# A residual's loads, activations' stores, two low parts of a column and one projection, moved to other queues, another engine, an earlier place

## The chip, the cores and the metric

One of the eight cores of a Trainium2 chip runs the whole program. Its engines are TensorE (PE, with PEld for its weight loads), VectorE (DVE), ScalarE (ACT), GpSimd (POOL) and SyncE (SP, which only issues DMAs). ScalarE and GpSimd can issue DMAs too, each on a queue of its own. The metric is the device time of one execution in microseconds (us), from the inputs in the chip's memory to the outputs in it.

## What is computed

Two transformer blocks on one sequence of 1024 tokens of width 1024, in float32. The change touches the second one:

```
h = rmsnorm(x, attn_norm)
q, k, v, g, gk_low, s5_u, rg_x, rg_gate = split(h @ w_in)
y_gla = gla_mixer(q, k, v, g, gk_low, ...)      # 4 heads, chunks of 64 tokens, decay per key feature
y_s5  = rmsnorm(s5_mixer(s5_u, ...))
y_rg  = rmsnorm(rglru_mixer(rg_x, rg_gate, ...))
x = x + concat(y_gla, y_s5, y_rg) @ w_out
h = rmsnorm(x, mlp_norm)
x = x + conv_ffn(h, w_up, conv_w, conv_b, w_down)
out = rmsnorm(x, final_norm)

def rglru_mixer(xr, gate, ...):
    xc = causal_dwconv(xr, conv_w, conv_b)
    r, i = sigmoid(xc @ w_a + b_a), sigmoid(xc @ w_x + b_x)      # per head
    a = exp(-8 * r * softplus(-lam))
    h_t = a_t * h_(t-1) + sqrt(1 - a_t**2) * i_t * xc_t
    return h * gelu(gate)

def conv_ffn(h, w_up, conv_w, conv_b, w_down):                   # 1024 -> 2 x 2816 -> 1024
    up, gv = split(h @ w_up)
    return (gelu(causal_dwconv(up, conv_w, conv_b)) * gv) @ w_down
```

The first block (two attentions, then a mixture of 16 experts) runs ahead of it.

## The kernel before, in words

A float32 product is made as three matmuls of rounded parts: each operand x is split into a high part h (rounded, a CAST or copy on ScalarE) and a low part l = x - h (a subtraction, most often on VectorE), and `mm3` issues h*h, h*l and l*h (lines 260 to 262). The high part is what PE waits for first, then the low part.

**Order.** The code is recorded operation by operation, and each engine then runs its own list in order; what stands in the lists is shown below where the change moves it. A DMA waits in its issuing engine's list, so whatever stands behind a waiting DMA waits too. Eight completion semaphores are taken in turn by the DMAs of the SP and ACT queues together: a DMA that takes one waits first until the previous DMA on it has landed.

**Mixers** (`mix_small`, from about 1100 to 1230 us of the span). PE makes the low-rank decay (`pgl`), then `gla_decays` for the first pair of heads: two products `pgk` (L1669), gz, Abs, Exp and Ln on ScalarE (L1670 to 1674), a scan on VectorE that makes gb, and a store of it to `qk_d` (L1678). Then come the eight products `prg` of the RG-LRU gates (L1538), each followed by a tanh into `rgg` on ScalarE (L1539), and RG-LRU's chain (L1544 to 1561). `gla_qk(0, 0)` and `gla_qk(0, 1)` are the projections of q and k for the first pair of heads: 48 matmuls each in two halves of 24, with a copy `qo` on ScalarE (L1689) and a store to `qk_d` on GpSimd's queue. Then S5's output product `pglu` (L1574) and `gla_decays` for the second pair. In `gla_out`, quad 0 loads q, k and gb back, takes exponentials `gx` on ScalarE (L1732), makes `gkd`, `QH`, `QT` on VectorE, and goes on with small matmuls (`pkd`, `sc`, `kv`, `po`). GpSimd clears QH, QT, KD and ST beforehand with twelve memsets (L1707).

**Handover** (`cols`, about 1395 to 1438 us). When a 128-token block j of the second half (j = 4 to 7) is normalised (`xn`, L269), PE transposes it (`pt`, L1894), and four sums of blocks are made with the rows of the first half (`rb`): t[0] (L1912), t[1] (L1913), t[2] (L1915) on VectorE, t[3] (L1916) on GpSimd. Each, and the block itself, is split: high part on ScalarE (L1899), low part on VectorE (L1900): XT2, XT3, XT1, XT4, X22. Up's first new product, `pb`, reads XT2.

**Up** (about 1433 to 1851 us). Seven products of half-size blocks take the place of eight, in 22 steps i; steps 2g and 2g + 1 make group g of eleven. `act(i)` multiplies gelu(up) by gv (L2220) into `ft` and stores parts of it to `act_d` (L2222, L2236, L2237); GpSimd makes sums of blocks (`block_sums`, L1980 to 1983) and stores them too (L2240 to 2242). GpSimd also makes the sums of the next weights (L2176 to 2184) and of Down's weights (L2227 to 2230).

**Down** (about 1851 to 2095 us). Seven products of eleven units. A unit is one tile `wraw` of two 256 KB loads, activations (L2033) and weights (L2034), then split into `whi` (L1999, ScalarE) and `wlo` (L2000, VectorE). The residual x3 comes into `res` in sixteen pieces of 256 KB (`piece`, L2025); product 0's call of `piece` after every second unit spreads them over the first products. The first CAST of Down writes into room that tiles of Up's activations held, so it waits for their last stores.

Of the kernel before, what the change touches and what calls it, by code (L numbers as in the profile page):

```python
# [7 lines left out]
F32 = mybir.dt.float32  # L8
# [4 lines left out]
OP = mybir.AluOpType  # L13
# [173 lines left out]
class K:  # L187
# [1232 lines left out]
    def mix_small(self, ps, st, XH, XL):  # L1420

        nc, a, V = self.nc, self.a, self.nc.vector
        from contextlib import ExitStack
        rg = self.pool(st, "rgwork")
        qk = self.pool(st, "qkwork", side="right")
# [78 lines left out]
        for q in range(4):  # L1504
# [13 lines left out]
            y = wb.tile([128, 4, 128], F32, tag="y5", name="y5", bufs=2)  # L1518
# [7 lines left out]
        gl, gu, gb, cm = self.gla_low(ps, qk, XH, XL)  # L1526
        self.gla_decays(ps, qk, 0, gl, gu, gb, cm)

        wr = rg.tile([128, 2, 2, 128], F32, name="rgw")
        nc.sync.dma_start(wr, a["rg_w"])  # L1530
        G = []
        for i in range(2):
            G.append([rg.tile([128, 1024], F32, tag=f"rgg{m}", name="rgg", bufs=2) for m in range(2)])
            for m in range(2):
                for n in range(2):
                    c = slice(512 * n, 512 * n + 512)
# [15 lines left out]
        for i in range(2):  # L1552
# [6 lines left out]
            V.tensor_tensor_scan(out=h, data0=t, data1=xc[i], initial=0.0, op0=OP.mult, op1=OP.add)  # L1559
            V.tensor_tensor(xc[i], h, GT[i], op=OP.mult)  # L1560
            nc.gpsimd.dma_start(self.yS[2 + i], xc[i])
        for t in range(2):
            self.gla_qk(ps, qk, XH, XL, 0, t)

        yf = [room("uf", "yf") for _ in range(2)]
        for i in range(2):
# [126 lines left out]
    def gla_out(self, ps, lw, ms, XH, XL):  # L1693
# [192 lines left out]
        def cols(xn, j):  # L1886


            c = slice(128 * (j % 4), 128 * (j % 4) + 128)
            pts = []  # L1890
            for q in range(2):
                pt = ps.tile([128, 4, 128], F32, tag="tr", name="pt", bufs=2)
                for d in range(4):
                    nc.tensor.transpose(pt[:, d], xn[:, 512 * q + 128 * d:512 * q + 128 * d + 128], self.ident)  # L1894
                pts.append(pt)

            def split(n, x):
                h, l = (t[:, :, c] for t in self.X[n])
                nc.scalar.copy(h, x)  # L1899
                V.tensor_tensor(l, x, h.bitcast(F32), op=OP.subtract)  # L1900
            if j < 4:
                r = wk.tile([128, 2, 4, 128], F32, tag="rb", name="rb", bufs=1)
                for q, n in enumerate(("11", "21")):
                    split(n, pts[q])
                    nc.scalar.copy(r[:, q], pts[q])
                nc.sync.dma_start(self.xr_d[j], r.rearrange("p q k t -> p (q k t)"))
                return
            b11, b21 = (raw[j][:, q] for q in range(2))
            p12, p22 = pts
            t = [ow.tile([128, 4, 128], F32, tag="yr", name="xt", bufs=4) for _ in range(4)]  # L1910
            nc.scalar.copy(t[3], p12)
            V.tensor_tensor(t[0], p12, b11, op=OP.subtract)  # L1912
            V.tensor_tensor(t[1], p22, t[0], op=OP.subtract)  # L1913
            split("T2", t[1])
            V.tensor_tensor(t[2], p22, t[3], op=OP.subtract)  # L1915
            nc.gpsimd.tensor_tensor(t[3], b21, t[1], op=OP.subtract)  # L1916
            split("T3", t[2])
            split("T1", t[0])
            split("T4", t[3])
            split("22", p22)  # L1920
            if j < 6:
                fetch(j + 2)
# [85 lines left out]
    def ffn_down(self, st, out):  # L2008
# [13 lines left out]
        def piece():  # L2022
            if pieces:
                j, c = pieces.pop(0)
                nc.sync.dma_start(res[:, j, c], self.x3_d[128 * j:128 * j + 128, c])  # L2025
        wdown = a["wdown"]
        second = {0: lambda g: wdown[g, :, n0], 1: lambda g: wdown[g + 11, :, n0], 2: lambda g: wdown[g + 11, :, n1]}
        for i, k in ((4, 0), (5, 1), (6, 2), (3, 3)):
# [21 lines left out]
        def product(i, P, start=False):  # L2050
            for g in range(11):
                w = unit(i, g)
                if g % 2:
                    piece()
                for t in range(4):
                    mms(P[t], w, t, start and g == 0, g == 10)
# [60 lines left out]
class Up:  # L2117
# [98 lines left out]
    def act(self, i):  # L2216
        nc, a, G, k, A = self.nc, self.a, self.nc.gpsimd, self.k, self.A
        t0, t1 = self.T0, self.T1
        g = i // 2
        nc.vector.tensor_tensor(A[i], A[i], self.U[i][1], op=OP.mult)  # L2220
        if i % 2 == 0:
            nc.sync.dma_start(k.act_d[0, g], A[i][:, t0])  # L2222

            r0, r1 = self.pair()
            nc.sync.dma_start(r0, a["wdown"][g])
            nc.sync.dma_start(r1, a["wdown"][g + 11])
            G.tensor_tensor(r0[:, t0], r0[:, t1], r0[:, t0], op=OP.subtract)  # L2227
            G.tensor_tensor(r0[:, t1], r1[:, t1], r0[:, t1], op=OP.subtract)
            G.tensor_tensor(r1[:, t1], r1[:, t1], r0[:, t0], op=OP.subtract)
            G.tensor_tensor(r1[:, t0], r1[:, t0], r1[:, t1], op=OP.subtract)  # L2230
            for x, n in ((r0, (0, 2)), (r1, (3, 1))):
                for c, m in zip((t0, t1), n):
                    nc.sync.dma_start(k.wdt_d[m, g], x[:, c])
            return
        x, y = A[i - 1], A[i]
        nc.sync.dma_start(k.act_d[1, g], y[:, t0])  # L2236
        nc.sync.dma_start(k.act_d[3, g], y[:, t1])  # L2237
        s12, s34 = self.pair()
        k.block_sums(G, s12, s34, x[:, t0], y[:, t0], x[:, t1], y[:, t1])
        G.dma_start(k.act_d[4:6, g].rearrange("i p c -> p i c"), s12.rearrange("p (i c) -> p i c", i=2))  # L2240
        G.dma_start(k.act_d[6, g], s34[:, t0])
        G.dma_start(k.act_d[2, g], s34[:, t1])
# [104 lines left out]
```

## Time and profile before

| | us |
|---|---|
| median of 3 runs | 2102.75 |
| lowest, highest | 2096.73, 2105.65 |
| the profiled execution | 2097.59 |
| its span, first to last instruction | 2095.7 |

The mean granted clock of TensorE in the profiled execution is 0.966 of full speed. The profile tells, for every engine, when each operation began and how long it took, how long the engine stood idle before it, and what ended that idle time (`[1.82 <-ACT rgg L1539]`: 1.82 us idle, until ScalarE's operation of line 1539 was done). An operation on PE of "x8" is eight that follow each other. L12 is line 12 of the kernel; SPq is the DMA queue of SP. The durations of matmuls are modelled and overlap; the spacing of their starts is what counts.

### The profile page before, as it was taken

The page shows a single profiled execution, that of the slowest core. Times are in us where ns is not written, and L with a number is a line of the kernel's source. Part 1 is how long each engine was busy: PE and PEld are TensorE (multiplying, and loading weights), DVE is VectorE, ACT ScalarE, POOL GpSimd, SP SyncE. Part 2 cuts the span into 40 slices and gives each one's busy share as a digit, 9 for nine tenths or more (in the row PEclk, how much of TensorE's full clock was granted, in tenths as well). Part 3 has the DMA queues.
Part 4 walks back from the last instruction along what each step waited for, and adds up shares of the span by engine and source line. Part 5 has one row for each costly group of instructions (what it writes and reads, how often), then busy time and mean ns, then how long its engine had stood idle before and what let it go on. Part 6 is the DMA issues. An engine that isn't in the chain of part 4 may idle for free. (4 is left out here: it accounts for less than half of the span.)

```text
span 2095.7 us, 27617 instructions
## 1 busy us (share of the span) xinstructions
PE 1925.1 (92%) x9481; PEld 1520.8 (73%) x9481; DVE 1318.6 (63%) x2668; ACT 928.2 (44%) x1645; POOL 718.3 (34%) x721
## 2 busy tenths in 40 slices
PE   8999999999898699986999898987999999959998
PEld 6877777776677577764887567766888888848886
DVE  4146667565667678756358468878667667634555
ACT  4245555444433467754422564354333333324344
POOL 2111112343432111105335144225777776720130
PEclk9999999999999799997999999998999999979999
DMA  6153322323432899966433257553344444357654
GB/s 241 60 128 100 100 73 69 111 76 101 157 97 76 264 306 322 317 207 231 156 86 68 71 201 231 174 191 136 132 180 151 146 169 148 139 208 243 194 191 170
DMA packets 162148, 336.42 MB, mean 161 GB/s; under 512 B 26352, under 2 KB 71696, under 8 KB 161488
## 3 DMA queue, kind: packets, MB, share of 16 engines
q1 hardware_dynamic: 140448, 264.84, 38.5%
q0 software_dynamic: 18848, 68.43, 10.0%
q10 hardware_dynamic: 2704, 1.31, 0.3%
q8 instruction: 77, 1.26, 0.3%
q14 instruction: 71, 0.58, 0.1%
HBM read 237.98 MB, written 87.03 MB: 155 GB/s over the span
## 5 line engine op out<-in xcount | busy, mean ns | idle before, releaser
L237 ACT CAST whi<-wraw 128x1024 fp32r<-128x1024 f32 x122 | 128.0, 1049 | 139.5 <-PE pp L261 46.6
L260 PE MATMUL pp<-XH,whi 128*128 128x512 f32 x416 | 167.7, 403 | 1.0 <-DVE kk L404 0.9
L261 PE MATMUL pp<-XL,whi 128*128 128x512 f32 x416 | 165.6, 398 | 0.0
L262 PE MATMUL pp<-XH,wlo 128*128 128x512 f32 x416 | 165.6, 398 | 0.0
L238 DVE TENSOR_TENSOR wlo<-wraw,whi 128x1024 fp32r<-128x1024 f32 x96 | 117.4, 1223 | 61.5 <-ACT whi L237 58.5
L2000 DVE TENSOR_TENSOR wlo<-wraw,whi 128x1024 fp32r<-128x1024 f32 x71 | 89.7, 1265 | 88.9 <-ACT whi L1999 87.2
L260 PE MATMUL pd<-whi 128*128 128x512 f32 x308 | 120.7, 393 | 23.2 <-ACT whi L1999 23.2
L2167 ACT CAST wh<-wr 128x1024 fp32r<-128x1024 f32 (+1 forms) x66 | 60.0, 909 | 163.3 <-PE pc L261 47.9
L1999 ACT CAST whi<-wraw 128x1024 fp32r<-128x1024 f32 x71 | 74.7, 1054 | 115.6 <-PE pd L262 90.9
L238 POOL TENSOR_TENSOR wlo<-wraw,whi 128x1024 fp32r<-128x1024 f32 x26 | 63.0, 2424 | 173.7 <-ACT whi L237 164.6
L261 PE MATMUL pd<-wlo,whi 128*128 128x512 f32 x308 | 120.9, 392 | 0.8 <-DVE wlo L2000 0.8
L262 PE MATMUL pd<-whi,wlo 128*128 128x512 f32 x308 | 120.5, 391 | 0.0
L1059 POOL DMA_INDIRECT xg<-xn_d,idx x25 | 31.2, 1247 | 187.6 <-PE pt L278 138.0
L260 PEld LDWEIGHTS pp<-XH,whi 128*128 128x128 f32 x416 | 78.9, 190 | 17.4 <-PE pp L262 1.8
L261 PEld LDWEIGHTS pp<-XL,whi 128*128 128x128 f32 x416 | 78.9, 190 | 16.2 <-issue 2.5
L262 PEld LDWEIGHTS pp<-XH,wlo 128*128 128x128 f32 x416 | 78.9, 190 | 14.8 <-issue 0.7
L2168 DVE TENSOR_TENSOR wl<-wr,wh 128x1024 fp32r<-128x1024 f32 (+1 forms) x66 | 83.1, 1260 | 7.7 <-ACT wh L2167 7.7
L260 PEld LDWEIGHTS pd<-whi 128*128 128x128 f32 x308 | 58.0, 189 | 36.9 <-ACT whi L1999 24.3
L531 ACT ACTIVATE PP<-PP,stat 128x256 f32<-128x256 f32 x128 | 64.5, 505 | 39.3 <-DVE stat L529 37.3
L2062 POOL TENSOR_TENSOR res<-res,p 128x512 f32<-128x512 f32 x12 | 23.7, 2011 | 144.0 <-DVE res L2060 144.0
L529 DVE CUSTOM_DVE_ANT_0 PP<-sp,bias 128x256 f32<-128x256 f32 x128 | 52.9, 422 | 25.4 <-PE sp L527 21.2
L261 PEld LDWEIGHTS pd<-wlo,whi 128*128 128x128 f32 x308 | 58.2, 189 | 14.2 <-DVE wlo L2000 2.1
(708 smaller groups left out, 5813.8 us busy)
## 6 DMA issues: line engine op xcount, KB each, us to landing
wraw<-in_wgu_dram SPq DMA_DIRECT2D x64, 512.0 KB, 5.5
wr<-in_wup_dram SPq DMA_DIRECT2D x44, 512.0 KB, 4.6
wraw<-act_d SPq DMA_DIRECT2D x77, 256.0 KB, 2.7
wraw<-in_wdn_dram SPq DMA_DIRECT2D x32, 512.0 KB, 5.3
fX<-in_wdown_dram SPq DMA_DIRECT2D x22, 512.0 KB, 4.2
wdt_d<-fX SPq DMA_DIRECT2D x44, 256.0 KB, 2.3
wraw<-wdt_d SPq DMA_DIRECT2D x44, 256.0 KB, 2.9
O<-ot SPq DMA_DIRECT2D x17, 512.0 KB, 4.7
```

The costliest lines, as they stand in the source:

```text
L237: nc.scalar.copy(hi, raw)
L238: (eng or nc.vector).tensor_tensor(lo, raw, hi.bitcast(F32), op=OP.subtract)
L260: nc.tensor.matmul(out, lh, rh, start=start, stop=False, **kw)
L261: nc.tensor.matmul(out, lh, rl, start=False, stop=False, **kw)
L262: nc.tensor.matmul(out, ll, rh, start=False, stop=stop, **kw)
L529: nc.vector.tensor_tensor_reduce(out=PP[j // 4][:, j % 4], in0=so, in1=bs, op0=OP.add, op1=OP.min, scale=1.0, scalar=3e38, accum_out=nm)
L531: nc.scalar.activation(PP[j // 4][:, j % 4], PP[j // 4][:, j % 4], AF.Exp, bias=nm, scale=-1.0, accum_out=stt[:, stj[0], 1, stj[1]:stj[1] ...
L1059: nc.gpsimd.indirect_dma_start(out=xg[0:n], out_offset=None, in_=self.xn_d, in_offset=bass.IndirectOffsetOnAxis(ap=idx[0:n, s, p:p + 1], a ...
L1999: nc.scalar.copy(h[:, 0:n], src)
L2000: nc.vector.tensor_tensor(l[:, 0:n], src, h[:, 0:n].bitcast(F32), op=OP.subtract)
L2167: self.nc.scalar.copy(h[:, 0:w], src)
L2168: self.nc.vector.tensor_tensor(l[:, 0:w], src, h[:, 0:w].bitcast(F32), op=OP.subtract)
```

## The change

1. In `mix_small`, `gla_qk(0, 0)` stands ahead of the RG-LRU gate products; `gla_qk(0, 1)` stays behind RG-LRU.
2. In `cols`, the low parts of XT1 and XT4 are made by GpSimd.
3. In `ffn_down`, the sixteen pieces of the residual are issued by ScalarE, and product 0 skips its first two calls of `piece`.
4. In `act`, the stores of `ft` (33 in all, 256 KB each) are issued by GpSimd.

```diff
--- before.py
+++ after.py
@@ -1526,6 +1526,7 @@
         gl, gu, gb, cm = self.gla_low(ps, qk, XH, XL)
         self.gla_decays(ps, qk, 0, gl, gu, gb, cm)
 
+        self.gla_qk(ps, qk, XH, XL, 0, 0)
         wr = rg.tile([128, 2, 2, 128], F32, name="rgw")
         nc.sync.dma_start(wr, a["rg_w"])
         G = []
@@ -1559,8 +1560,7 @@
             V.tensor_tensor_scan(out=h, data0=t, data1=xc[i], initial=0.0, op0=OP.mult, op1=OP.add)
             V.tensor_tensor(xc[i], h, GT[i], op=OP.mult)
             nc.gpsimd.dma_start(self.yS[2 + i], xc[i])
-        for t in range(2):
-            self.gla_qk(ps, qk, XH, XL, 0, t)
+        self.gla_qk(ps, qk, XH, XL, 0, 1)
 
         yf = [room("uf", "yf") for _ in range(2)]
         for i in range(2):
@@ -1894,10 +1894,10 @@
                     nc.tensor.transpose(pt[:, d], xn[:, 512 * q + 128 * d:512 * q + 128 * d + 128], self.ident)
                 pts.append(pt)
 
-            def split(n, x):
+            def split(n, x, eng=V):
                 h, l = (t[:, :, c] for t in self.X[n])
                 nc.scalar.copy(h, x)
-                V.tensor_tensor(l, x, h.bitcast(F32), op=OP.subtract)
+                eng.tensor_tensor(l, x, h.bitcast(F32), op=OP.subtract)
             if j < 4:
                 r = wk.tile([128, 2, 4, 128], F32, tag="rb", name="rb", bufs=1)
                 for q, n in enumerate(("11", "21")):
@@ -1915,8 +1915,8 @@
             V.tensor_tensor(t[2], p22, t[3], op=OP.subtract)
             nc.gpsimd.tensor_tensor(t[3], b21, t[1], op=OP.subtract)
             split("T3", t[2])
-            split("T1", t[0])
-            split("T4", t[3])
+            split("T1", t[0], nc.gpsimd)
+            split("T4", t[3], nc.gpsimd)
             split("22", p22)
             if j < 6:
                 fetch(j + 2)
@@ -2022,7 +2022,7 @@
         def piece():
             if pieces:
                 j, c = pieces.pop(0)
-                nc.sync.dma_start(res[:, j, c], self.x3_d[128 * j:128 * j + 128, c])
+                nc.scalar.dma_start(res[:, j, c], self.x3_d[128 * j:128 * j + 128, c])
         wdown = a["wdown"]
         second = {0: lambda g: wdown[g, :, n0], 1: lambda g: wdown[g + 11, :, n0], 2: lambda g: wdown[g + 11, :, n1]}
         for i, k in ((4, 0), (5, 1), (6, 2), (3, 3)):
@@ -2050,7 +2050,7 @@
         def product(i, P, start=False):
             for g in range(11):
                 w = unit(i, g)
-                if g % 2:
+                if g % 2 and (i or g > 4):
                     piece()
                 for t in range(4):
                     mms(P[t], w, t, start and g == 0, g == 10)
@@ -2219,7 +2219,7 @@
         g = i // 2
         nc.vector.tensor_tensor(A[i], A[i], self.U[i][1], op=OP.mult)
         if i % 2 == 0:
-            nc.sync.dma_start(k.act_d[0, g], A[i][:, t0])
+            G.dma_start(k.act_d[0, g], A[i][:, t0])
 
             r0, r1 = self.pair()
             nc.sync.dma_start(r0, a["wdown"][g])
@@ -2233,8 +2233,8 @@
                     nc.sync.dma_start(k.wdt_d[m, g], x[:, c])
             return
         x, y = A[i - 1], A[i]
-        nc.sync.dma_start(k.act_d[1, g], y[:, t0])
-        nc.sync.dma_start(k.act_d[3, g], y[:, t1])
+        G.dma_start(k.act_d[1, g], y[:, t0])
+        G.dma_start(k.act_d[3, g], y[:, t1])
         s12, s34 = self.pair()
         k.block_sums(G, s12, s34, x[:, t0], y[:, t0], x[:, t1], y[:, t1])
         G.dma_start(k.act_d[4:6, g].rearrange("i p c -> p i c"), s12.rearrange("p (i c) -> p i c", i=2))
```

Where instructions stand, word for word from the two programs' lists.

PE in the mixers, before (`pgk` are the decays' products, `prg` the RG-LRU gates', `pp` the projection of q):

```order
L1649 MATMUL pgl<-XL_12110,gkw 16x512
L1669 MATMUL pgk<-gl,gu 128x512
L1538 MATMUL prg<-xc,rgw 128x512
L1669 MATMUL pgk<-gl,gu 128x512
L1538 MATMUL prg<-xc,rgw 128x512 x7
L1574 MATMUL pglu<-yf,wglu 128x512
L260 MATMUL pp<-XH_12109,whi 128x512
L261 MATMUL pp<-XL_12110,whi 128x512
L262 MATMUL pp<-XH_12109,wlo 128x512
```

and now, each of the two dotted places being the rest of 24 matmuls `pp`:

```order
L1649 MATMUL pgl<-XL_12110,gkw 16x512
L1669 MATMUL pgk<-gl,gu 128x512
L260 MATMUL pp<-XH_12109,whi 128x512
L261 MATMUL pp<-XL_12110,whi 128x512
L262 MATMUL pp<-XH_12109,wlo 128x512
...
L1669 MATMUL pgk<-gl,gu 128x512
...
L1539 MATMUL prg<-xc,rgw 128x512 x8
L1574 MATMUL pglu<-yf,wglu 128x512
```

The 48 matmuls of `gla_qk(0, 0)`, which stood behind `pglu`, now stand in two halves behind the two `pgk`, and all eight `prg` follow them.

VectorE in the handover, the last column, before:

```order
L1912 TENSOR_TENSOR xt<-pt,rb_15944 128x512
L1913 TENSOR_TENSOR xt<-pt,xt 128x512
L1915 TENSOR_TENSOR xt<-pt,xt 128x512
L1900 TENSOR_TENSOR XT1l<-xt,XT1h 128x4x128
L1900 TENSOR_TENSOR XT2l<-xt,XT2h 128x4x128
L1900 TENSOR_TENSOR XT3l<-xt,XT3h 128x4x128
L1900 TENSOR_TENSOR XT4l<-xt,XT4h 128x4x128
L1900 TENSOR_TENSOR X22l<-pt,X22h 128x4x128
L2263 TENSOR_TENSOR up<-pf,gv 128x512
```

and GpSimd now, from the column j = 6 on:

```order
L1900 TENSOR_TENSOR XT1l<-xt,XT1h 128x4x128
L1916 TENSOR_TENSOR xt<-rb_15876,xt 128x512
L1900 TENSOR_TENSOR XT4l<-xt,XT4h 128x4x128
L1900 TENSOR_TENSOR XT1l<-xt,XT1h 128x4x128
L1916 TENSOR_TENSOR xt<-rb_15944,xt 128x512
L1900 TENSOR_TENSOR XT4l<-xt,XT4h 128x4x128
L2176 TENSOR_TENSOR fS<-wr_16113 128x512
```

VectorE's list has lost XT1l and XT4l of each column; on GpSimd XT1l stands ahead of L1916, XT4l behind it, and both ahead of the sums of the next weights.

SP at the end of Up and the start of Down, before:

```order
L2222 DMA act_d<-ft 128x512
L2025 DMA res_19139<-x_d 128x512 x3
L2236 DMA act_d<-ft 128x512
L2237 DMA act_d<-ft 128x512
L2025 DMA res_19139<-x_d 128x512 x7
L2033 DMA wraw<-act_d 128x512
L2034 DMA wraw<-in_wdown_dram 128x512
```

and ScalarE there, now (three rows of Up, the pieces, Down's first casts):

```order
L2283 COPY up<-pa 128x512
L2208 ACTIVATE ft<-up,fcv 128x1024
L2211 ACTIVATE ft<-ft 128x1024
L2025 DMA res_19139<-x_d 128x512 x16
L1999 CAST whi<-wraw 128x1024 x15
L2066 COPY p_19140<-pd 128x512 x4
```

On SP the stores of `ft` and the ten pieces that stood ahead of Down's first unit (L2033, L2034) are gone, and its list goes from the last store of Up's weights to the final norm's load and then that unit; on ScalarE all sixteen pieces stand between the last gelu of Up and the first CAST of Down. With the semaphores taken in turn, the ninth piece waits for the first one's landing, the sixteenth for the eleventh's, and the two loads of unit 0 for those of pieces 6 and 8.

## Rows read from the trace of the kernel before

**Rows 1.** Waits of PE by line, 1100 to 1450: us in total, times, longest.

```profile
PE pt L1894 <- DVE X22l L1900: 9.0, 3, 4.3
PE pt L1894 <- DVE xn L269: 4.0, 1, 4.0
PE pb L260 <- ACT XT2h L1899: 1.4, 1, 1.4
PE pb L261 <- DVE XT2l L1900: 1.4, 1, 1.4
```

**Rows 2.** Stretches: us, busy us of PE, PEld, DVE, ACT, POOL, clock, DMA, GB/s.

```profile
1180.00:1190.00 10.00, 6.76 (x15) 3.46 (x16) 5.86 (x4) 9.50 (x11) 0.59 (x1) 0.66 0.13 52
1420.00:1430.00 10.00, 3.31 (x8) 2.16 (x9) 9.33 (x12) 6.17 (x11) 4.04 (x3) 0.50 0.57 205
1440.00:1838.00 398.00, 398.00 (x1731) 324.79 (x1730) 269.35 (x248) 147.18 (x166) 285.09 (x190) 1.00 0.41 149
```

**Rows 3.** PE's timeline, mixers: start us, us, operation, [idle before, what ended it].

```profile
1174.20 3.81 PE L1538 MATMUL prg<-xc,rgw 128*128 128x512 f32 x8 [1.15 <-ACT gz L1670]
1179.83 1.13 PE L1538 MATMUL prg<-xc,rgw 128*128 128x512 f32 x2 [1.82 <-ACT rgg L1539]
1184.19 2.08 PE L1538 MATMUL prg<-xc,rgw 128*128 128x512 f32 x2 [3.24 <-ACT rgg L1539]
1210.27 0.39 PE L262 MATMUL pp<-XH,wlo 128*128 128x512 f32 x1
1210.50 2.74 PE L1574 MATMUL pglu<-yf,wglu 128*128 128x512 f32 x6
1231.77 0.44 PE L1749 MATMUL pkd<-ident,gkd 128*128 128x128 f32 x2 [1.62 <-DVE gkd L1738]
```

**Rows 4.** Timelines of ACT, DVE and POOL, mixers: three operations.

```profile
1186.31 0.69 ACT L1539 ACTIVATE rgg<-prg,rgsp 128x512 f32<-128x512 f32 x1 [0.43 <-PE prg L1538]
1227.53 2.29 DVE L1677 TENSOR_TENSOR_SCAN gb<-cm,gz 128x1024 f32<-128x1024 f32 x1
1223.38 0.59 POOL L1707 MEMSET ST<- 128x256 f32 x2
```

**Rows 5.** Timelines of DVE and POOL, handover: the last column.

```profile
1426.15 0.68 DVE L1900 TENSOR_TENSOR XT1l<-xt,XT1h 128x512 fp32r<-128x512 f32 x1
1426.75 1.76 DVE L1900 TENSOR_TENSOR XT2l<-xt,XT2h 128x512 fp32r<-128x512 f32 x1
1426.47 1.50 POOL L1916 TENSOR_TENSOR xt<-rb,xt 128x512 f32<-128x512 f32 x1 [5.14 <-ACT XT2h L1899]
```

**Rows 6.** Timeline of all engines, start of Down (SPq is SP's DMA queue).

```profile
1851.30 1.27 SPq L2025 DMA_DIRECT2D res<-x_d  x3
1856.13 1.06 ACT L2211 ACTIVATE ft<-ft 128x1024 f32<-128x1024 f32 x1 [2.73 <-DVE ft L2210]
1858.47 0.32 SPq L2236 DMA_DIRECT2D act_d<-ft  x1
1863.63 0.67 SPq L2034 DMA_DIRECT2D wraw<-in_wdown_dram  x1
1864.68 0.56 POOL L2242 DMA_DIRECT2D act_d<-fX  x1
1873.19 2.01 ACT L1999 CAST whi<-wraw 128x1024 fp32r<-128x1024 f32 x2 [16.00 <-DMA wraw<-in_wdown_dram]
1874.29 1.22 PE L260 MATMUL pd<-whi 128*128 128x512 f32 x2 [23.02 <-ACT whi L1999]
1879.92 1.23 DVE L2000 TENSOR_TENSOR wlo<-wraw,whi 128x1024 fp32r<-128x1024 f32 x1 [0.79 <-ACT whi L1999]
```

**Rows 7.** DMA in 40 slices of 1 us, from 1840 to 1880.

```profile
GB/s 160 0 262 182 342 16 0 0 0 0 0 0 213 285 252 37 0 0 0 266 307 320 172 184 301 309 295 391 397 422 410 402 402 416 395 111 72 361 166 315
```

**Rows 8.** Timelines of POOL and ACT in Up: a sum and its cast.

```profile
1727.71 1.28 POOL L2184 TENSOR_TENSOR wr<-wr,fS 128x512 f32<-128x512 f32 x1
1732.48 0.62 ACT L2167 CAST wh<-wr 128x512 fp32r<-128x512 f32 x1 [1.67 <-PE pb L261]
```

## The prediction

> **What bounds the kernel now.** I read the waits of TensorE (PE) first, because PE carries the span: a change gains only where PE stands still or is slow, or loses where it is made to. From the second block's mixers to the start of Up, its longest waits are those for the handover's columns [rows 1] and, in several pieces, for RG-LRU [rows 3]; in Up it does not wait at all, 398 us busy of 398 [rows 2]; at the start of Down it has one wait of 23.0 us for the first cast [rows 6]. The table by stretches then gives the clock: 0.50 in 1420–1430, 0.66 in 1180–1190 [rows 2], so what follows such a gap runs at the lower level (1.2 GHz) for some matmuls. Only then the timelines, engine by engine: for the mixers [rows 3, 4], one column of the handover [rows 5], the start of Down [rows 6, 7], one pair of Up [rows 8]. The change touches exactly these three gaps, and Up.
>
> **Part A, the order in the mixers.** Before, the eight RG-LRU gate products (prg) follow the decay products at once, and PE waits between them for ScalarE: 1.15 + 1.82 + 3.24 = 6.2 us [rows 3]; the one after the longest wait runs cold. Now 24 matmuls stand behind each of the two pgk products: 24 x 0.233 us (the pitch at the end of this block, 1210.27 against 1210.50 for the next row) = 5.6 us each, 11.2 us in all, which cover the time in which ScalarE issues stores and does gz, Abs, Exp and Ln. So up to 6.2 us of waiting goes. Late next is ScalarE: it must now also do two qo copies before its Exp, and the RG-LRU chain, whose last tanh was at 1186.31, starts behind 11.2 us of matmuls; by my replay the tanh comes at 1194 to 1196. That chain isn't what quad 0 waits for: quad 0 needs the second gz chain, and its gx and gkd stand behind that on ScalarE and VectorE, where gb's scan ended at 1229.8 [rows 4]; PE had matmuls to do until 1230 and waited 1.62 us [rows 3]. That second chain begins only when ScalarE is through RG-LRU's functions and their table loads. My replay brings it 0 to 2 us forward, not 6. On GpSimd eleven of the memsets of QH, QT, KD and ST now stand behind the second store of gb, so quad 0's writes to them come later than they might, by up to 3.6 us (twelve memsets of 0.3 us, the last two in [rows 4]). I take **-2 us**, bounds -6.2 (all waits gone, nothing given back) and +2 (quad 0 waits for the memsets, which eat the 1.6 that was PE's wait and some more).
>
> **Part B, two low parts of a column on GpSimd.** DVE does eight 128x512 operations a column, one every 0.60 us when alone (1426.15 to 1426.75), busy 9.3 of 10 us in 1420–1430 [rows 2, 5]; PE waits there for X22l and xn, 9.0 + 4.0 us, and for XT2's two parts, 2.8 us [rows 1]. The change takes two operations from DVE: 1.2 us a column, three columns (j = 5, 6, 7) on the chain that ends in the first product with XT2, so -3.6 us at best. On GpSimd the two cost up to 1.5 us each (L1916, of the same shape, took 1.50 us), and one of them stands ahead of L1916. What it gives back is in the same rows: XT2l, both of whose inputs are in SBUF, took 1.76 us while GpSimd ran L1916 (1426.47 to 1427.97), against a pitch of 0.60. More GpSimd work in the same stretch means more such meetings. With two meetings a column, each (1.69 - 0.60) = 1.1 us, three columns give 6.6 - 3.6 = +3 us; with none, -3.6. XT2l already meets L1916 once in these columns, and XT1l, which ran just before it, kept 0.68 us, so I count about half a new meeting a column (3 x 0.5 x 1.1 = 1.6): **-2 us**, bounds -3.6 and +3. The Trainium skill's page "SBUF — State Buffer", section "Who interferes with whom", speaks against this part: a VectorE operation with two SBUF inputs and a GpSimd operation that reads SBUF exclude each other for the whole instruction. By it each new GpSimd operation could hold a VectorE subtraction once, which would be the +3 above; the trace's 1.76 us agrees that such a meeting costs.
>
> **Part C, the start of Down.** Before, ten residual pieces (L2025) and two stores stand ahead of the first unit on SP; the unit's second half was issued at 1863.63 and the first cast began at 1873.19, PE at 1874.29 [rows 6]. The name of the change would free the unit of them. But the order shows all sixteen pieces on ScalarE's queue *ahead of the first cast of Down*, and since eight completion semaphores are shared by the SP and ACT queues, piece 9 waits for piece 1's landing and piece 16 for piece 11's; unit 0's own loads wait for pieces 6 and 8. So the first cast stands behind eleven landed pieces, and the first piece is issued only when ScalarE has done its last gelu, 1856.13 + 1.06 = 1857.2, where SP issued three at 1851.30. Bytes: 256 KB (0.262 MB) each. Moved per us from 1859 (0.5 us behind the first issue of this burst, at 1858.47): about 0.27 MB in the first eight slices (266 to 295 GB/s), about 0.40 in the next eight (391 to 395) [rows 7]. Eleven pieces, six stores of activations and unit 0 are 19 x 0.262 = 4.98 MB: 8 us for 2.15 MB and 7.0 us for the rest, from 1857.7 (0.5 us behind the first issue) to 1872.7, and the cast 0.5 us later (piece 16's issue): 0 us against before. If all of units 0 to 3 comes in before piece 11 (25 transfers of the 30, 6.6 MB), it is 1876.7, +4. Below: eleven pieces alone (2.88 MB) land at 1867.5, the cast comes at 1868 and PE 5 us earlier than before. That end needs the stores and unit 0 to come ahead of their queue, though the last of the stores is issued at 1864.68 and GpSimd now has two more issues ahead of it, 1.1 us. I take **+1 us**, bounds -5 and +4. Units 1 to 3 don't starve at this rate: all 30 transfers (7.86 MB) are in at 1857.7 + 8 + 14.1 = 1879.8, cast and low part (1.0 + 1.2 us [rows 6]) done at 1882.1, when PE needs unit 3 only at about 1884.7 (three units of twelve matmuls stand before it, 8.2 us at full clock and some 2 more for the cold first one).
>
> What a page says on this: by "DMA: Bandwidth & Descriptors" of the Trainium skill, section "Queues, rings and completion order", each DMA engine alternates between queues at the granularity of packets. By that, a queue of its own gives unit 0 a share and no more bytes; this trace has no stretch with two full hardware queues that would show it.
>
> **Part D, the stores in Up on GpSimd.** 33 issues move to GpSimd at 0.56 us (the same kind of issue there, [rows 6]): 18.5 us on an engine that is busy 285 of 398 us in Up [rows 2], so it fits on the whole. SP's waits for these stores vanish, but PE waited for none of it. What stands behind the two issues is GpSimd's sums of the activations and of the next weights; the sums come 1.1 us later, and where I looked the sum was done at 1729.0 and its cast began at 1732.5 [rows 8], so there is room for it. **0 us**, bounds 0 and +3 (a late sum in some of the eleven pairs).
>
> **The sum.** -2 - 2 + 1 + 0 = -3 us. Against the profiled execution, 2097.59 us (span 2095.7), that is 2094.6 us. The median of the runs, 2102.75, lies 5.2 us higher; I carry the difference over to it: 2102.75 - 3 = 2099.75, **2100 us**. About 0.5%, 10.5 us, is what a measurement of this kernel can tell from no change; no term alone reaches it.
>
> **The rivals.**
> Rival 1, everything arrives: the units are freed (C = -5), the two operations meet nothing (B = -3.6), the waits of the mixers go whole (A = -6.2): -14.8 us, **2088 us**. For it: each gap is real and PE has work behind each. Against it: the cast behind the pieces, and quad 0's own chain. Chance 0.12.
> Rival 2, the first units starve behind the residual: three queues with reads and writes together hold the rate at the level of the first eight slices or below. At 0.22 MB/us, between the lowest two slices (172 and 184) and their mean, the 7.86 MB take 35.7 us, to 1893.4; unit 3 is ready at 1895.7 instead of 1884.7, **+11 us**; with A and B giving nothing, **2114 us**. It costs from the point where the mean rate of the 30 transfers falls under 7.86 MB / (1882.4 - 1857.7 us) = 0.32 MB/us; my own sum has 0.36. For it: before, 1862–1864 shows just that fall, and all of the residual now comes in this stretch, sixteen pieces for ten. Chance 0.08.
> Rival 3, the ports eat the handover and the order in the mixers gives nothing: A = 0, B = +3, C = +4, D = 0: +7 us, **2110 us**, still within 0.5%. For it: 1.76 us against 0.60. Chance 0.12.
> Forecast: 0.68, from about -9 to +5 us around its -3.
> The change also might not do what it says: SP's queue does stand with Down's units alone in the order, but their start hangs on ACT's queue by the semaphores; that is in C.
>
> **How the numbers follow.** Faster by over 0.5% is rival 1, 0.12. Slower by over 0.5% is rival 2, 0.08. Within 0.5% are the forecast and rival 3, 0.80. The range leaves out the outer half of rival 1 and rival 2: from 2102.75 - 13.8 = 2089 to 2102.75 + 8.3 = 2111.
>
> **What would show it.** Right for A: no wait of PE for rgg, and prg as one block behind the second pgk; wrong if PE's wait before quad 0 grows from 1.6 us to over 5. Right for B: PE's waits for X22l and xn shorter by about 1 us each, and more VectorE subtractions of 1.7 us; wrong if xn or XT2l is awaited longer than before. Right for C: sixteen pieces on ScalarE's queue that run from 1857 to about 1872, the first cast within 2 us of 1873; wrong if it comes before 1870 or after 1877, or if PE waits again for units 1 to 3. Right for D: PE still 398 of 398 us in Up. A clock that differs over long stretches would make the whole comparison wrong.

## The result, and the profile after

| | median, us | lowest to highest, us | runs |
|---|---|---|---|
| before | 2096.73 | 2092.48 to 2105.65 | 9 |
| changed | 2116.97 | 2107.30 to 2122.62 | 9 |

The ratio is 1.0084, with an interval of 1.006 to 1.0108: the change makes the kernel 0.84% slower, some 18 us, and the time lies above the stated range of 2089 to 2111. The profiled execution has a span of 2110.2 us against 2095.7. One of all the runs told of below, of the changed kernel without part D, was slow (9450 us) and is left out of its median.

Where the 14.5 us of the two spans lie, read from PE's timelines as the lengths between the first starts of products (or the last, where it says so), in us:

| stretch | before | changed | part A alone | part B alone | part C alone | part D alone |
|---|---|---|---|---|---|---|
| span's start to pgl (the change touches nothing here) | 1161.2 | 1155.8 | 1160.4 | 1158.2 | 1160.6 | 1158.5 |
| pgl to pkd: mixers | 70.6 | 74.7 | 73.9 | 70.5 | 70.2 | 70.5 |
| pkd to last po: quads, output projection | 169.7 | 171.1 | 173.4 | 171.8 | 169.3 | 170.6 |
| last po to pb: handover | 24.9 | 24.4 | 24.9 | 24.5 | 24.8 | 24.9 |
| pb to last pc: Up | 424.5 | **437.3** | 424.6 | 423.3 | 424.6 | **438.6** |
| last pc to pd: gap ahead of Down | 23.4 | 24.7 | 23.4 | 22.9 | 24.1 | 23.5 |
| pd to the span's end: Down | 221.4 | 222.3 | 222.0 | 222.7 | 222.8 | 223.4 |

The first row varies by several us between kernels that run the same code there; the third by up to four. In the first row the changed kernel happens to be 5.4 us ahead, so the other rows lose 20 us together. The loss stands in Up, 12.8 us, where the forecast had nothing; the mixers lose 4.1 us where it had a gain of 2.

The waits of PE in the changed kernel (PE's operation, what it waited for, us in total, times, longest): from the mixers to the handover, in Up, and from the start of Down. For the handover, [rows 1] has the same waits before.

```profile
PE pt L1894 <- DVE xn L269: 5.4, 1, 5.4
PE pp L260 <- ACT qo L1689: 5.3, 1, 5.3
PE prg L1539 <- ACT rgg L1540: 3.4, 2, 3.2
PE pt L1894 <- DVE xt L1912: 3.2, 1, 3.2
PE pt L1894 <- DVE X22l L1900: 2.9, 1, 2.9
PE pb L260 <- ACT XT2h L1899: 1.5, 1, 1.5
PE pb L261 <- DVE XT2l L1900: 1.0, 1, 1.0
...
PE pb L260 <- DVE gv L2287: 11.1, 10, 1.2
...
PE pd L260 <- ACT whi L1999: 24.5, 2, 24.3
```

Up now has a wait that it did not have: ten times about 1.1 us, once in each group but the last, for VectorE's gv, which empties a bank of `pb` (L2287). Before, PE was busy 398 of 398 us [rows 2]. From one group's sums to the next group's it is now 40.1 us instead of 38.7: the 1.1 us of the wait and 0.3 us that the profile puts down to no wait.

What makes gv late: the groups of VectorE's low parts of the weights' sums in Up (line, operation, how many, busy us and mean ns of one, idle before), before and then changed:

```profile
L2168 DVE TENSOR_TENSOR wl<-fS,wh 128x1024 fp32r<-128x1024 f32 x20 | 25.8, 1289 | 23.0 <-ACT wh L2167 23.0
```

```profile
L2168 DVE TENSOR_TENSOR wl<-fS,wh 128x1024 fp32r<-128x1024 f32 x20 | 68.7, 3433 | 15.9 <-ACT wh L2167 15.9
```

Its mean rose from 1.29 to 3.43 us: one in each group takes about 5 us now, the other 1.2 to 2.3. One group shows how. First before (start us, us, engine, line, operation): VectorE's L2168 and GpSimd's sums of the activations.

```profile
1667.25 1.23 DVE L2168 TENSOR_TENSOR wl<-fS,wh 128x1024 fp32r<-128x1024 f32 x1 [1.32 <-ACT wh L2167]
1669.09 0.69 DVE L2287 TENSOR_TENSOR gv<-pb,gv 128x512 f32<-128x512 f32 x1 [0.62 <-PE pb L262]
...
1666.01 1.29 POOL L1980 TENSOR_TENSOR fX<-ft 128x512 f32<-128x512 f32 x1 [3.57 <-DVE ft L2220]
1667.26 2.37 POOL L1982 TENSOR_TENSOR fX<-ft 128x512 f32<-128x512 f32 x1
```

and the same group changed:

```profile
1672.59 4.95 DVE L2168 TENSOR_TENSOR wl<-fS,wh 128x1024 fp32r<-128x1024 f32 x1 [1.33 <-ACT wh L2167]
1677.46 0.68 DVE L2287 TENSOR_TENSOR gv<-pb,gv 128x512 f32<-128x512 f32 x1
...
1671.56 0.56 POOL L2236 DMA_DIRECT2D act_d<-ft  x1 [3.79 <-DVE ft L2220]
1672.11 0.54 POOL L2237 DMA_DIRECT2D act_d<-ft  x1
1672.67 1.30 POOL L1980 TENSOR_TENSOR fX<-ft 128x512 f32<-128x512 f32 x1
1673.92 1.28 POOL L1982 TENSOR_TENSOR fX<-ft 128x512 f32<-128x512 f32 x1
1675.17 1.28 POOL L1981 TENSOR_TENSOR fX<-fX,ft 128x512 f32<-128x512 f32 x1
1676.40 0.56 POOL L2241 DMA_DIRECT2D act_d<-fX  x1
...
1678.19 0.50 PE L260 MATMUL pb<-XT4h,wh 128*128 128x512 f32 x1 [0.99 <-DVE gv L2287]
```

Before, L2168 came up as the first sum ended, ran its 1.23 us, and GpSimd's second sum took 2.37 instead of 1.29. Now the sums come 1.1 us later, behind two DMA issues; L2168 comes up together with the first of them and is done only after the third: 3 x 1.25 + 1.2 = 4.95 us. VectorE's next operation, gv, waited 0.62 us for PE before; now PE waits 0.99 us for it.

### The profile page after: what moved, and what is told of

Its sections match the earlier page's. It is cut to its first block, busy times and chain, and to the rows that moved or that the text cites. A ratio compares the mean times of both kernels' runs of the same rounds, so it can differ in the third digit from the quotient of the medians.

```text
span 2110.2 us, 27626 instructions
## 1 busy us (share of the span) xinstructions
PE 1930.2 (91%) x9481; PEld 1521.6 (72%) x9481; DVE 1372.2 (65%) x2660; ACT 925.3 (44%) x1643; POOL 749.4 (36%) x762
## 3 DMA queue, kind: packets, MB, share of 16 engines
q8 instruction: 77, 1.26, 0.2%
## 4 chain that ended last, share of the span: by engine, by line
PE 36%; DVE 8%; DMA 3%; issue 3%; ACT 3%; POOL 2%; SPq 0%; ACTq 0%; POOLq 0%; DVEq 0%
PE pd L260 3%; PE pd L261 3%; PE pd L262 3%; PE pb L260 3%; PE pb L261 2%; PE pb L262 2%; DVE wl L2168 2%; PE pa L261 2%; PE pa L260 2%; PE pa L262 2%; PE pc L260 1%; PE pc L262 1%; PE pc L261 1%; PE pvg L260 1%; PE pvg L262 1%
## 5 line engine op out<-in xcount | busy, mean ns | idle before, releaser
L260 PE MATMUL pd<-whi 128*128 128x512 f32 x308 | 120.9, 394 | 25.3 <-ACT whi L1999 24.5
L260 PEld LDWEIGHTS pp<-XH,whi 128*128 128x128 f32 x416 | 79.8, 192 | 24.5 <-ACT qo L1689 5.7
L2168 DVE TENSOR_TENSOR wl<-wr,wh 128x1024 fp32r<-128x1024 f32 (+1 forms) x66 | 89.3, 1354 | 6.6 <-ACT wh L2167 5.4
L2168 DVE TENSOR_TENSOR wl<-fS,wh 128x1024 fp32r<-128x1024 f32 x22 | 71.1, 3232 | 17.5 <-ACT wh L2167 17.5
L2062 POOL TENSOR_TENSOR res<-res,p 128x512 f32<-128x512 f32 x12 | 23.7, 2008 | 144.6 <-DVE res L2060 144.6
L281 DVE TENSOR_TENSOR XL<-pt,XH 128x512 fp32r<-128x512 f32 x32 | 20.7, 686 | 76.2 <-ACT XH L280 76.1
```

Of the source, the lines that this page charges most:

```text
L260: nc.tensor.matmul(out, lh, rh, start=start, stop=False, **kw)
L2062: nc.gpsimd.tensor_tensor(r, r, p1[:, t], op=OP.add)
L2168: self.nc.vector.tensor_tensor(l[:, 0:w], src, h[:, 0:w].bitcast(F32), op=OP.subtract)
```

## The experiments

All times below are medians against runs of the kernel before on the same chip (2097.4 to 2098.5 us there); the ratio carries its 95% interval, and the us that follow it are worked out from the ratio (the difference of the two medians is up to 2.3 us off that).

### Which part

Part D alone (the edit to `act` of the diff):

> The kernel before with part D alone: the 33 stores of ft on GpSimd's queue, two of them ahead of each group's sums. Theory 1 (two issues of 0.56 us shift GpSimd's three sums so that they run against VectorE's low part of fS): TensorE waits for gv (L2287) some 11 us in ten groups, the low part wl<-fS (L2168) takes about 3.4 us instead of 1.29, time +11 to +13 us against before. Rival a (the loss is made by the four parts together, or by another one): within 4 us of before.

Measured 2112.51 us, ratio 1.0066 (1.005 to 1.0083), +14 us. PE's first wait in Up there:

```profile
PE pb L260 <- DVE gv L2287: 11.1, 10, 1.2
```

The changed kernel without part D:

> The changed kernel with part D undone: parts A, B and C alone, the stores of ft on SP again. Theory 1: no wait for gv in Up, wl<-fS at 1.3 us, time 11 to 13 us below the changed kernel, that is 0 to +6 us against before. Rival a: as slow as the changed kernel, +15 us.

Measured 2100.91 us, 1.0015 (1.0002 to 1.0028), +3 us, and no wait in Up. So part D makes most of the loss, by itself.

### What in part D

The two stores of odd steps behind the sums, still on GpSimd's queue:

```
         s12, s34 = self.pair()
         k.block_sums(G, s12, s34, ...)
         ... three stores of the sums ...
+        G.dma_start(k.act_d[1, g], y[:, t0])
+        G.dma_start(k.act_d[3, g], y[:, t1])
```

> Part D alone, with the two stores of odd steps issued by GpSimd behind the group's sums and their stores instead of ahead of them: as many DMA issues on GpSimd, the sums where they were. Theory 1: within 3 us of before, no wait for gv of over 1 us in all. Rival b (it is the DMA issues on GpSimd themselves, 33 more of them, or their queue): +11 us, as in part D alone.

Measured 2096.29 us, 0.9988 (0.9974 to 1.0003): the same queue and the same 33 issues cost nothing. Rival b falls in its plain form. Next, the place of the sums without any store moved, by N copies of one column of `ft` (shown in one form for all; which of the two tiles comes first differs between the runs):

```
         s12, s34 = self.pair()
+        for n in range(N):
+            s = (s12, s34)[n % 2]
+            G.tensor_copy(s[:, 0:1], y[:, n:n + 1])
         k.block_sums(G, s12, s34, ...)
```

Two copies:

> The kernel before with no store moved: two copies of one column of ft by GpSimd stand ahead of each group's sums and put them off by about 1.1 to 1.3 us. All else stands as before, GpSimd's order of the weights' sums too. Theory 1: +8 to +13 us, the wait for gv back, wl<-fS at about 3.4 us. Rival b (the DMA issues themselves) and rival c (GpSimd's last weight sum L2184, which part D also moves ahead of L2228): within 3 us of before.

Measured 1.0007 (0.9994 to 1.0021). The copies put the sums off by 0.26 us only, so the moment was not reached. Eight:

> As the run with two one-column copies ahead of each group's sums, but with eight of them (0.135 us each, as that run showed), so that the sums begin 1.1 us later than before, about as much later as with part D's two DMA issues; no store is moved and GpSimd's order is that of before. Theory 1 (what counts is when the sums begin against VectorE's wl<-fS): TensorE waits for gv again, wl<-fS near 3.4 us, +8 to +13 us. Rivals b and c (the DMA issues themselves; the place of L2184): within 3 us of before.

Measured 1.0008 (0.9991 to 1.0025): a miss. L2168 came up 0.2 us after the first sum and waited for that sum alone:

```profile
1662.51 2.11 DVE L2168 TENSOR_TENSOR wl<-fS,wh 128x1024 fp32r<-128x1024 f32 x1 [1.32 <-ACT wh L2167]
...
1662.25 1.29 POOL L1980 TENSOR_TENSOR fX<-ft 128x512 f32<-128x512 f32 x1
1663.49 2.29 POOL L1982 TENSOR_TENSOR fX<-ft 128x512 f32<-128x512 f32 x1
```

Eleven:

> As the run with eight copies, with eleven: the sums then begin some 0.15 us after VectorE's wl<-fS was to begin, the place they have with part D's two DMA issues (there -0.08 to -0.17 us in nine groups of ten), where eight copies still left wl<-fS 0.2 us behind the sums' start. No store is moved. Theory 1 (phase alone): wl<-fS waits for all three sums, about 5 us instead of 1.23 in the ten groups, +8 to +13 us. Rival b (a DMA issue right ahead of the sums is needed): wl<-fS at most 2.4 us, within 3 us of before.

Measured 1.001 (0.9994 to 1.0026): a miss of theory 1 again. In two groups L2168 stood 0.12 us ahead of the first sum, as in part D, and kept 1.23 us; in the other eight the sums began only after it. The moment alone does not do it (the sums then ran behind copies, with no DMA issue ahead). Part D with five copies between its issues and the sums:

> Part D alone, the two DMA issues ahead of the sums, and five one-column copies between them and the sums (0.6 us), so that wl<-fS begins clearly ahead of the sums. Theory 1: wl<-fS keeps about 1.3 to 1.6 us and the sums wait for it instead; within 3 us of before. Rival b (the DMA issues themselves hold VectorE back): wl<-fS at 4 us or more in the ten groups and +11 us or more.

Measured 0.9988 (0.9973 to 1.0003); L2168 came up at the end of the issues, 1.71 us ahead of the sums, took 1.23 us, and the copies waited for it (1.59 us for five):

```profile
1667.69 1.23 DVE L2168 TENSOR_TENSOR wl<-fS,wh 128x1024 fp32r<-128x1024 f32 x1 [1.21 <-ACT wh L2167]
...
1667.33 0.54 POOL L2237 DMA_DIRECT2D act_d<-ft  x1
1667.86 1.59 POOL L2241 COPY fX<-ft 128x1 f32<-128x1 f32 x5
```

This kernel has GpSimd's list in part D's order, with L2184 ahead of L2228, and loses nothing, so rival c falls. With one copy there:

> Part D alone with its two DMA issues ahead of the sums and one one-column copy (0.13 us) between them and the sums. If it takes a DMA issue directly ahead of the sums for them to go first: wl<-fS at most 2.5 us, within 4 us of before. If it takes only the issues in the 1.3 us ahead and the moment: wl<-fS about 5 us in the ten groups, +11 us or more.

Measured 2113.71 us, 1.0064 (1.0039 to 1.009): L2168 took 5.08 to 5.16 us in all ten groups though a copy stood between:

```profile
1673.57 5.08 DVE L2168 TENSOR_TENSOR wl<-fS,wh 128x1024 fp32r<-128x1024 f32 x1 [1.32 <-ACT wh L2167]
...
1673.63 0.20 POOL L2241 COPY fX<-ft 128x1 f32<-128x1 f32 x1
```

Against the end of the second issue, L2168 came up at the same moment with no copy, one and five: 0.08 to 0.18 us ahead of it. What differs is what stands behind the issue. Last, the two stores as one DMA, directly ahead of the sums:

```
-        G.dma_start(k.act_d[1, g], y[:, t0])
-        G.dma_start(k.act_d[3, g], y[:, t1])
+        G.dma_start(k.act_d[1:4:2, g].rearrange("i p c -> p i c"),
+                    y.rearrange("p (i c) -> p i c", i=2))
```

> Part D alone with the two stores of odd steps as one DMA of 512 KB, directly ahead of the sums: the issue takes 0.73 us instead of 1.10, so that wl<-fS begins some 0.2 us behind the sums' start instead of 0.1 ahead. If a DMA issue directly ahead is enough at any such moment: wl<-fS about 4.6 us, +8 us or more. If wl<-fS must come up while the issue runs: it waits for the first sum alone, 2.1 us, within 4 us of before.

Measured 2108.24 us, 1.0053 (1.0032 to 1.0074), and one group of it:

```profile
1667.57 4.61 DVE L2168 TENSOR_TENSOR wl<-fS,wh 128x1024 fp32r<-128x1024 f32 x1 [1.32 <-ACT wh L2167]
...
1666.54 0.73 POOL L2236 DMA_DIRECT2D act_d<-ft  x1 [3.79 <-DVE ft L2220]
1667.29 1.30 POOL L1980 TENSOR_TENSOR fX<-ft 128x512 f32<-128x512 f32 x1
1668.53 1.31 POOL L1982 TENSOR_TENSOR fX<-ft 128x512 f32<-128x512 f32 x1
1669.79 1.30 POOL L1981 TENSOR_TENSOR fX<-fX,ft 128x512 f32<-128x512 f32 x1
```

Beside the run with eight copies this is the clean pair: L2168 comes up 0.2 to 0.3 us after the first sum's start in both; behind copies it waits for one sum (2.1 us), behind a DMA issue for all three (4.6 us). All ten groups of each kernel, the start of L2168 against that of the first sum L1980 (plus: later):

| ahead of the sums | L2168 against L1980, us | L2168 took, us |
|---|---|---|
| nothing (before) | +1.16 to +1.24 | 1.22 to 1.23 |
| 2 copies | +0.92 to +0.99 | 1.38 to 1.47 |
| 8 copies | +0.18 to +0.26 | 2.11 to 2.20 |
| 11 copies | -0.11 and -0.12, eight times -1.2 | 1.22 to 1.24 |
| part D alone, stores behind the sums | +1.16 to +1.26 | 1.23, once 2.37 |
| two issues (part D alone) | -0.08 to -0.16 | 4.96 to 5.05 |
| two issues (changed) | -0.08 to -0.17, once +0.14 | 4.74 to 5.05 |
| two issues, 1 copy | -0.20 to -0.28 | 5.08 to 5.16 |
| one issue of 0.73 us | +0.19 to +0.28, once -0.05 | 4.61 to 4.94 |
| two issues, 5 copies | -1.71 and -1.72 | 1.22 to 1.23 |

What follows, for the cases run: the loss came when a DMA issue of GpSimd stood directly or one copy ahead of the sums and L2168 came up between that issue's last 0.2 us and the first sum's first 0.3 us; with five copies between issue and sums it did not come. The moment without an issue, or an issue elsewhere, cost VectorE at most 1.2 us, and PE did not wait for gv. Why a DMA issue ahead lets three sums pass where otherwise one does, the runs do not show; this stays open.

The cure tried on the changed kernel, the stores behind the sums and all else as changed:

> The changed kernel with one edit: the two stores of odd steps issued by GpSimd behind the group's sums. Theory 1 (the loss of the change is those issues ahead of the sums): no wait for gv in Up, 11 to 14 us below the changed kernel, 0 to +4 us against before. Rival a (the parts together lose it): 5 us or less below the changed kernel.

Measured 2104.84 us, 1.0024 (1.0008 to 1.0041): +5 us against before, some 12 below the changed kernel, and no wait for gv. It bears theory 1 out in the changed kernel too: the issues ahead of the sums make most of the loss. What is left fits part A's +4 alone, below.

### The mixers

> The kernel before with part A alone. Theory 2 (quad 0's first loads, gmask and gq, wait for the room that RG-LRU's chain leaves, and part A makes that chain end later): the load of gmask is issued right behind the last L1561 of RG-LRU, 5 to 8 us later than at 1210.6, and the time is +2 to +5 us. Rival (the forecast's: quad 0 waits for the second gz chain alone): -2 to 0 us.

Measured 2103.63 us, 1.0018 (1.0001 to 1.0036), +4 us. The load of gmask on SP and VectorE's last operation of RG-LRU, first before, then with part A alone:

```profile
1210.56 0.33 SPq L1702 DMA_DIRECT2D gmask<-in_gmask_dram  x1
1211.06 0.59 SPq L1722 DMA_DIRECT2D gq<-qk_d  x1
...
1209.27 1.23 DVE L1560 TENSOR_TENSOR xc<-XR,GT 128x1024 f32<-128x1024 f32 x1
```

```profile
1222.92 0.33 SPq L1702 DMA_DIRECT2D gmask<-in_gmask_dram  x1
1223.41 0.59 SPq L1722 DMA_DIRECT2D gq<-qk_d  x1
...
1221.54 1.31 DVE L1561 TENSOR_TENSOR xc<-XR,GT 128x1024 f32<-128x1024 f32 x1
```

gmask goes out 0.06 us behind the product's end in the one and 0.07 in the other, and 0.08 in the changed kernel (1218.04, 1218.12): quad 0's loads wait for the room that RG-LRU's chain leaves. Counted from pgl, whose own start varies (first row of the table), the chain ends at 49.3 us before, at 62.4 with part A alone and at 62.3 in the changed kernel: 13 us later in both, more than the 5 to 8 expected. Its price, on ScalarE before and then on ScalarE and PE in the changed kernel:

```profile
1227.55 0.42 ACT L1732 ACTIVATE gx<-gq 128x256 f32<-128x256 f32 x1
```

```profile
1225.45 0.42 ACT L1732 ACTIVATE gx<-gq 128x256 f32<-128x256 f32 x1 [6.93 <-DMA gq<-qk_d]
1225.78 1.07 ACT L1689 ACTIVATE qo<-pp 128x512 f32<-128x512 f32 x2
...
1226.41 0.80 PE L260 MATMUL pp<-XH,whi 128*128 128x512 f32 x1 [5.30 <-ACT qo L1689]
```

Before, gx did not wait: it ran 16.5 us behind the issue of the load of gq. In the changed kernel ScalarE was ready for gx 3.6 us earlier, counted from pgl (162.8 instead of 166.4), but stood 6.9 us until gq had landed; the copies that empty PE's banks stand behind gx, and PE waits 5.3 us. The matmuls behind that wait ran at a granted clock of 0.50, the 1.2 GHz level (1226.4 to 1229.5, against 1.00 before in 1226 to 1231), 0.43 us apart instead of 0.23. The other way round, the first pair's decays behind RG-LRU's gates:

```
-        self.gla_decays(ps, qk, 0, gl, gu, gb, cm)
         wr = rg.tile([128, 2, 2, 128], F32, name="rgw")
         ... the gates ...
+        self.gla_decays(ps, qk, 0, gl, gu, gb, cm)
         ... the rest of RG-LRU ...
```

> The other way round: the decays of the first pair of heads stand behind RG-LRU's gates instead of ahead of them, so that RG-LRU's chain ends earlier; the projection stays where it was before. Theory 2: gmask is issued 4 to 8 us earlier than at 1210.6, quad 0 begins some us earlier, time -2 to -6 us. Rival (the chain's end does not matter, the gz chain of the first pair does): 0 to +4 us, since that chain is now later.

Measured 2107.81 us, 1.0039 (1.0022 to 1.0056), +8 us: a miss. RG-LRU's chain did not end earlier but at 1216.2, since two gate products had moved so far ahead that PE waited 7.9 us for their input and 6.4 us for a bank behind them. gmask went out at 1216.25, again right behind the chain, so the loads' wait holds, but the run says nothing on what an earlier end would give. Counted from pgl the chain ended where it did before (49.9 us against 49.3), gx again did not wait, and pkd still came 5.3 us sooner (65.3 instead of 70.6): as long as the loads come in time, it is not the chain that holds quad 0. The stretches ahead of pgl and behind pkd lost more than that.

### The handover and the start of Down

> The kernel before with part B alone, XT1's and XT4's low parts on GpSimd. By the forecast's step: TensorE's waits for X22l and xn 3 us shorter together, time -2 us (bounds -3.6 and +3). Rival (the two operations on GpSimd hold VectorE's other subtractions and delay L1916): 0 to +3 us, more low parts on VectorE of 1.6 us and over.

Measured 2095.62 us, 0.999 (0.9976 to 1.0004), -2 us: not told from nothing. PE's waits there:

```profile
PE pt L1894 <- DVE xn L269: 5.5, 1, 5.5
PE pt L1894 <- DVE xt L1912: 3.7, 2, 2.8
PE pt L1894 <- DVE X22l L1900: 2.9, 1, 2.9
```

The wait for X22l fell from 9.0 to 2.9 us, but those for xn and xt rose, 4.0 and 0.9 to 5.5 and 3.7; the handover is 0.4 us shorter.

> The kernel before with part C alone. By the forecast's step: the first cast of Down stands behind sixteen pieces on ScalarE, TensorE's wait there 24 us instead of 23.0, time +1 us (bounds -5 and +4).

Measured 2099.56 us, 1.0002 (0.9987 to 1.0017); PE's wait ahead of Down was 23.7 us instead of 23.0. In the changed kernel, ScalarE at the start of Down:

```profile
1868.53 13.71 ACTq L2025 DMA_DIRECT2D res<-x_d  x16
1886.80 1.04 ACT L1999 CAST whi<-wraw 128x1024 fp32r<-128x1024 f32 x1 [17.30 <-DMA res<-x_d]
```

Sixteen pieces in 13.7 us, the first cast behind them. The residual held back instead, a piece only after a unit's cast:

```
-                nc.sync.dma_start(res[:, j, c], ...)
+                nc.gpsimd.tensor_copy(res[:, j, c.start:c.start + 1], h[:, 0:1].bitcast(F32))
+                nc.gpsimd.dma_start(res[:, j, c], ...)
-                if g % 2:
-                    piece()
+                if g % 2 and (i or g > 4):
+                    piece(w[0])
```

> The kernel before with part C made so that the first units stand alone: the residual's pieces are issued by GpSimd, each behind a copy of one column of the unit's high part into its place, so that none is loaded before that unit's cast, from product 0's unit 5 on. Theory 3 (it is the residual's bytes and pieces ahead of the first cast that keep it at 1873): the first cast comes when the last stores of Up's activations have landed, at 1867 to 1869, time -4 to -6 us. Rival (the stores themselves and the units take as long without the residual, or the pieces come too late for the sums L2060): -1 to +3 us.

Measured 2097.14 us, 0.9993 (0.9974 to 1.0012): a miss, within the noise of nothing. The first cast waited for the last stores of the activations' sums:

```profile
1867.31 0.56 POOL L2243 DMA_DIRECT2D act_d<-fX  x1
1874.55 3.88 ACT L1999 CAST whi<-wraw 128x1024 fp32r<-128x1024 f32 x4 [14.74 <-DMA act_d<-fX]
```

issued at 1867.3 and landed by 1874.5. The first four units' eight loads now stood in the residual's place beside them; that they made the stores late is not shown. PE's wait was 21.7 us instead of 23.0.

### Three parts together

> Part B, part D with the two stores behind the sums, and the residual's pieces issued by GpSimd behind the casts from product 0's unit 5 on; the order in the mixers is that of before. By the single runs (-2.5 for the late stores, -1 for the pieces, -2 to 0 for part B): -2 to -6 us against before. Rival (the parts disturb each other's timing on GpSimd): 0 or slower.

Measured 2093.51 us, 0.9972 (0.9958 to 0.9987), -6 us (-4 by the medians): faster than both kernels, though none of the three alone could be told from nothing. PE's wait ahead of Down is 18.1 us there, 5 less than before; which part gives it was not run apart.

## Why the prediction was wrong

The total, -3 us forecast, +18 measured (+14.5 between the profiles, +20 without the row ahead of pgl). The base of the forecast, 2102.75 us from three runs, was 6 us above the median of the nine, so the range lay high and the time still came above it.

**Part D, 0 forecast, +14 measured: this is the step that failed.** I counted the 33 issues against GpSimd's idle time, and the lateness of its sums against their readers, and found room for both. The sums are in time, and GpSimd does have the room. What I did not ask is what the sums would run beside once they came 1.1 us later. Part B priced such a meeting, 1.1 us, from XT2l [rows 5]; the same rule was to be put to VectorE's subtraction in Up, 1.24 us behind the first sum before, in ten groups. By that price a meeting would have cost VectorE 1.1 us at most (eight copies cost it 0.9, and PE did not wait for gv). That several operations of GpSimd pass one after another behind a DMA issue stood in no row that I read, but it does stand in the trace of before, in the first block:

```profile
523.80 2.30 DVE L598 TENSOR_SCALAR PQ<-PQ,statn 128x384 f32<-128x384 f32 x1
...
523.30 0.58 POOL L227 DMA_DIRECT2D wraw<-in_wout_dram  x1
523.89 0.75 POOL L762 TENSOR_TENSOR yr<-yr 128x256 f32<-128x256 f32 x1
524.60 1.27 POOL L760 TENSOR_TENSOR YL<-yr,YH 128x512 fp32r<-128x512 f32 x1
```

L598 has a median of 0.42 us; here it came up in the last 0.1 us of GpSimd's issue and ended only after both operations. The bound of +3 was so too narrow for a part that moves something in ten groups of a stage without a wait: 1.1 us of PE in each is 11.

**Part A, -2 forecast, +4 alone.** The failed step is the sentence that RG-LRU's chain isn't what quad 0 waits for. It was true of the kernel before, where gq was loaded long ahead of gx, but the room of quad 0's first loads hangs on the chain's last product; the trace of before had it, gmask 0.06 us behind the product. I forecast the chain's tanh 8 to 10 us later and put no price on it; the chain ended 13 us later, and the loads became what quad 0 waits for. That ScalarE comes forward was right (3.6 us, 0 to 2 forecast). The waits for rgg did not go (3.4 of 5.1 us stayed), and the sign of being wrong came, a wait of 5.3 us ahead of quad 0. The memsets behind gb's store show in no wait of PE.

**Part B, -2 forecast, -2 (-5 to +1) alone.** Within its bounds; the table by stretches gives 0.4 us in the handover. The half meeting a column was too few: XT2l took 1.8 us in each of the last three columns (before, 1.1 in one of them), XT3l 1.75 and 1.19 in two. The Trainium skill's rule ("SBUF — State Buffer", section "Who interferes with whom") speaks of two such operations excluding each other; the traces agree here (1.8 us for XT2l) and in Up: with eight copies ahead, L2168 took 0.9 us longer, the rest of one GpSimd sum. Where a DMA issue stood ahead of the sums, L2168 took 3.7 us longer, for three of them; that is more than that rule's one instruction, and the measurement decides.

**Part C, +1 forecast, +0.4 (-2.7 to +3.6) alone, +1.3 us of gap in the changed kernel.** Right: sixteen pieces ahead of the first cast, over 13.7 us, the cast 18.3 us behind the last gelu's start where it was 17.1 before, and no starving of units 1 to 3. My low end, the units freed at once, was wrong in its reason: without the residual ahead, the first cast waited for the stores of the sums instead, and came only some 1.3 us sooner.

**The rivals.** Slower by over 0.5% had 0.08, for a starving of Down's first units; the mechanism that came was the one of rival 3, VectorE and GpSimd in each other's way, in Up instead of the handover.

## What to carry to other kernels

Moving DMA issues to an engine that has room is not free because it has room: each issue shifts what stands behind it, and in a loop without slack the shift is paid in every turn. Before such a move, look at what the shifted operations will run beside, above all two-input operations of VectorE beside GpSimd's, and put the issues behind the work that others meet. And where a step is made later, look for loads that wait for its tiles' room, not only for readers of its results.

## What the runs showed of the hardware

A subtraction of VectorE with both inputs in SBUF that came up during one of GpSimd's 128x512 sums waited for the rest of that sum and then ran (0.2 us in: 2.1 us instead of 1.23; 0.95 us in: 1.4), and a sum that came up during the subtraction waited for it (2.3 instead of 1.29). With a DMA issue of GpSimd just ahead of three sums, the same subtraction ended only after all three and took 4.6 to 5.2 us, in four kernels and all ten groups of each, also when it came up 0.1 us ahead of the first. Five one-column copies between undid that, one did not. An operation with one tile as input (L598, 128x384) met two GpSimd operations behind a DMA issue in the same way, 2.3 us instead of 0.42. Why, the runs do not show.
